# Low query parts of the prompt attention: from 64 rows in a double buffer to 128 rows, half of them zero, in a single one

## The chip, the cores and the metric

One core of one Trainium2 chip. The metric is the device time of one execution in microseconds, the median of the runs of the kernel. Each core has a matrix engine, TensorE (PE), with its own queue of weight loads (PEld), a vector engine, VectorE (DVE), a scalar engine, ScalarE (ACT), GpSimd (POOL), and SyncE (SP), which here only issues DMAs. Matrix products read SBUF (128 partitions, called rows below) and write PSUM, which this part of the kernel uses as eight banks of 128 x 512 numbers of four bytes.

## The reference, cut to what matters

One inference step of one decoder layer: a prompt of 1024 positions and 64 sample positions share the weights. A SwiGLU half step, a combined input projection, two attentions A and B over its output, their branches and an output projection, a cross attention over memory keys, a second SwiGLU half step and a final norm. The change touches the two attentions of the prompt:

```python
# A: 8 query heads over 2 key heads, keys at distances 0..128, a learned sink per head
# B: 12 query heads = 3 groups x 4 key heads; group (window, dilation) in (128,1), (512,4), (2048,16)
sc = jnp.einsum('nbqkgd,nbjkd->nbkgqj', qb, kk, preferred_element_type=jnp.float32) * ATTN_SCALE
sc = jnp.where(mask[None, :, None, None], sc, -jnp.inf)
lse = jax.nn.logsumexp(sc, axis=-1)
p = jnp.exp(sc - lse[..., None]).astype(v.dtype)
o = jnp.einsum('nbkgqj,nbjkd->nbqkgd', p, vv, preferred_element_type=jnp.float32)
```

A head has 64 features, so a score sums 64 products.

## The kernel before, in words

All matrix products run on operands split into a high and a low part of a rounded float type (F32R); a product of two numbers is the sum of high x high, high x low and low x high. `mm3` (lines 228 to 231) issues the three for the large layers. A planner (the tile framework, with a simulated time line) sets the order of the instructions on each engine: by the priority of their emission, among those that are ready in its simulation; `early(p)` emits under the earlier priority p. Engines then run their own lists in that order and wait on semaphores. Buffers of a pool with n `bufs` are reused in turn and a new use waits for the last reader of the old.

The prompt attention (lines 796 to 1034) runs over 24 units: u // 8 is the kind (0: A over its two key heads; 1 and 2: B, two key heads at a time), u % 8 the block i of 128 queries. Per unit there are two jobs, one per key head j.

- `kv_prep` (line 828) brings keys and values of 512 positions from DRAM (`zscr`), transposes the keys on PE and puts them in `KT`: 128 rows per key head, for j = 0 high parts on rows 0 to 63 and low parts on rows 64 to 127, for j = 1 the other way round.
- `q_load` (line 851) loads the raw queries of a unit by one DMA into one of four slots `qr`, which the keys and values use too.
- `q_prep` (line 860) transposes them on PE into a PSUM bank `pT` (one of three, which the jobs use for the probabilities too). For each head half e, ACT copies the high part twice (lines 873 and 874), so that a head's high part stands on rows 0 to 63 and again on rows 64 to 127; DVE subtracts it from the bank and gets the low part (lines 879 and 881), on 64 rows alone, those of the key head. All of it lies in `QT`, two buffers of 12 parts of 128 columns: 8 of high parts, 4 of low parts.
- `qk` (line 884) makes the scores of 128 queries and up to 512 keys in two products: line 890 contracts 128 rows, [high; high] with [high; low] of the keys; line 891 adds low queries x high keys over 64 rows.
- `job_a` (line 898) and `job_b` (line 941): the scores go through DVE with the mask and the maximum (`ttr`, line 463) into `Sm` (three buffers), ACT takes the exponential, in B POOL adds the groups, DVE scales, PE transposes the probabilities into `pT` (lines 930 and 982), ACT and DVE split them into `PT` (three buffers; `split2`, lines 225 and 226), and PE multiplies them with the values (`pO`).
- The unit loop (lines 1012 to 1027) emits the next unit's `q_load` and `q_prep` before the jobs of the present one, so they have priority over these.

PE's list is filled up with the gates' products (`gate`, line 801; 36 units of 24 products, tile `pf`), emitted behind all of it, some of them tied to follow a given job (`GATE_AFTER`).

Of the kernel before, what the change touches and what calls it, by code (L numbers as in the profile page):

```python
# [10 lines left out]
F32R = mybir.dt.float32r  # L11
# [23 lines left out]
G0 = 18  # L35
# Which of the attention's jobs each unit of gate work follows: their share of the units, by their length.
_SHARE = np.cumsum([1.0, 4.0] + [1.0] * 14 + ([2.0] + [1.0] * 15) * 2)
# [11 lines left out]
class Weights:  # L49
    """The stream of weight tiles in the order of their use: loads run ahead, then each is split  # L50
    exactly into a high and a low part of float32r."""

# [47 lines left out]
def trunk(ctx, tc, A, O, dbg=None):  # L100
# [8 lines left out]
    class early:  # L109
        """What is emitted inside goes before the work emitted since priority p where both are ready."""  # L110

# [9 lines left out]

    # ---------------------------------------------------------------- weights, in order of use
    entries = []
# [70 lines left out]

    # ---------------------------------------------------------------- what lives throughout
    dr = ctx.enter_context(pool(name="dr", bufs=1, space=DRAM))
# [36 lines left out]
    def finish_rstd(dst, ssum, n):  # L233
        """dst = 1/sqrt(ssum / D + eps), with a Newton step behind the square root."""
        sd = small.tile([128, 9], F32, name="sd", tag="sd")
        v = small.tile([128, 9], F32, name="vv", tag="vv")
        t = small.tile([128, 9], F32, name="tt", tag="tt")
        S.activation(sd[:, :n], ssum, AF.Sqrt, scale=1.0 / D, bias=epst)
        V.tensor_scalar(v[:, :n], ssum, 1.0 / D, EPS, op0=ALU.mult, op1=ALU.add)
        V.reciprocal(sd[:, :n], sd[:, :n])  # L240
        V.tensor_tensor(t[:, :n], sd[:, :n], sd[:, :n], op=ALU.mult)
        V.tensor_tensor(t[:, :n], t[:, :n], v[:, :n], op=ALU.mult)
        V.tensor_scalar(t[:, :n], t[:, :n], -0.5, 1.5, op0=ALU.mult, op1=ALU.add)
        V.tensor_tensor(dst, sd[:, :n], t[:, :n], op=ALU.mult)
# [33 lines left out]

    # ---------------------------------------------------------------- feed-forward
    def ffn(pre, x, psp, fp, stats, after, order=(0, 1, 2), before=lambda c: None, at=(5, 6)):  # L280
# [85 lines left out]

    # ================================================================ start, first feed-forward
    ss = const.tile([128, 1152], F32, name="ss")
# [64 lines left out]

    # ================================================================ input projection and attention
    def stop(name):
# [4 lines left out]
    with ExitStack() as ph:  # L440
# [24 lines left out]

        # ------------------------------------------------------------ projection, position-major
        m1 = ph.enter_context(ExitStack())
# [59 lines left out]

        # ------------------------------------------------------------ sample
        with early(p_m1), ExitStack() as sp_:
            # ---- scores of the widest dilation: each key serves one position  # L530
            ST = sq.tile([128, 2, 8, 2, 8], F32, name="ST")
# [17 lines left out]

            # ---- B  # L550
            with ExitStack() as sb_:
# [135 lines left out]

            # ---- A
            with pool("da") as da:
# [27 lines left out]
                for hf in range(2):  # L717
# [4 lines left out]
                    split2(KH[:, bs, 0:128], KL[:, bs, 0:128], pk[:, :].rearrange("p (b k) -> p b k", b=4))  # L722
                # per b a block of 128 query columns (b % 2, j, g, t), zero elsewhere
                QH = da.tile([128, 4, 2, 2, 2, 4, 8], F32R, name="QH")
# [70 lines left out]

        # ------------------------------------------------------------ prompt
        ap = ph.enter_context(pool("ap"))
        marks, gw = [], {}

        # ------------------------------------------------------------ gates: the work to fill in with  # L800
        def gate(u):
# [21 lines left out]
        with ExitStack() as pp:  # L823
            qe = pp.enter_context(pool("qe"))
            qp = pp.enter_context(pool("qp"))
            halves = [0]

            def kv_prep(kc, vc, hf):
                """Half of the keys of two heads, transposed: head 0 [high; low], head 1 [low; high]; values."""
                rows = slice(hf * 512, hf * 512 + 512)  # L830
# [20 lines left out]
            def q_load(i, c0, ng):  # L851
                """The queries of ng groups and two key heads, in pairs of heads."""
                qr = qe.tile([128, 4, 128], F32, name="qr", tag="qr", bufs=4)
# [6 lines left out]
            def q_prep(qr, ng):  # L860
                """Per head [high; high] over 128 rows, and per pair of heads the low parts."""
                QT = qp.tile([128, 12, 128], F32R, name="QT", tag="QT", bufs=2)
                p = bank(pst, "pT")
# [3 lines left out]
                for e in range(2):  # L867
# [7 lines left out]
                    if ng == 4:  # L875
                        for j in range(2):
                            lo = QT[j * 64:j * 64 + 64, 8:12].rearrange("p (g e) c -> p g e c", e=2)[:, :, e]
                            gs = slice(2 * j, 2 * j + 2)
                            V.tensor_tensor(lo, pv_[r, gs], _b(hi[r, gs]), op=ALU.subtract)
                    else:  # L880
                        V.tensor_tensor(QT[r, 2 * ng:3 * ng], pv_[r], _b(hi[r]), op=ALU.subtract)
                return QT

            def qk(out, QT, ng, g, j, KV, k0, n):
                r = slice(j * 64, j * 64 + 64)
                for hf in range(2):
                    a, e = max(k0, hf * 512), min(k0 + n, hf * 512 + 512)
                    if a < e:
                        o, KT, c = out[:, a - k0:e - k0], KV[hf][0], slice(a - hf * 512, e - hf * 512)
                        PE.matmul(o, QT[:, j * ng + g], KT[:, j, c], start=True, stop=False)  # L890
                        PE.matmul(o, QT[r, 2 * ng + g], KT[r, j, c], start=False, stop=True)  # L891

# [3 lines left out]

            # ---- A: sliding window with sinks
            def job_a(i, j, QT, oA, KV):
# [40 lines left out]

            # ---- B: three dilations over shared keys, two key heads at a time  # L940
            def job_b(i, j, QT, oB, KV):
# [49 lines left out]

            def qs(u):
                ph_, i = u // 8, u % 8
                if ph_ == 0:
                    return q_prep(q_load(i, 0, 4), 4)
                return q_prep(q_load(i, 640 + ph_ * 128, 3), 3)

            def kv(ph_, hf):
# [11 lines left out]
                                                ap=[[0, 128], [1, 8]]))  # L1010
            QTs = [qs(0)]
            for u in range(24):
                ph_, i = divmod(u, 8)
                if u < 23:
                    QTs.append(qs(u + 1))
                if ph_ < 2 and i == 6:
# [5 lines left out]
                for j in range(2):  # L1022
                    (job_b if ph_ else job_a)(i, j, QTs[u], ob, KVs[ph_])
                os_, t = oscr[i // 3], slice(i % 3 * 128, i % 3 * 128 + 128)
# [10 lines left out]

    # ================================================================ branches and the output projection
    xph = ctx.enter_context(ExitStack())
# [133 lines left out]

    # ================================================================ cross attention
    MS = 128.0 ** -0.5
    with ExitStack() as ph:
# [8 lines left out]
        def gbank(both):  # L1183
            """A bank for a product over all tokens; where nothing else runs, those of the scores too."""
            turn[0] = (turn[0] + 1) % 3
# [126 lines left out]
        def sample():  # L1312
            with ExitStack() as sx:
# [4 lines left out]
                with pool("dk", 2) as dk:  # L1318
# [3 lines left out]
                    for h in range(4):  # L1322
# [26 lines left out]
                        V.tensor_scalar(P[:, h], P[:, h], Z[:, h:h + 1], None, op0=ALU.mult)  # L1349
                # per b a block of 128 columns (b % 2, high or low part, h, t), zero elsewhere  # L1350
                PT = dm.tile([128, 2, 4, 2, 2, 2, 4, 8], F32R, name="PTm")
# [58 lines left out]

    # ================================================================ second feed-forward, final norm
    with ExitStack() as ph:
# [20 lines left out]
        def half(t, hf, tag):  # L1433
            """Half of the features of 128 positions, back to position-major, times the gain; their squares."""
            rows = 128 if t < 8 else 64
# [29 lines left out]
        def last(c):  # L1465
            """The second halves of the last positions and what is left of their norm, straight from PSUM."""
            ps = []
# [36 lines left out]
def constants():  # L1504
    """Tables that depend on the shapes alone."""
    f = np.float32
# [19 lines left out]
    c["c_mask"] = np.concatenate([band(2, 1, 128), band(5, 4, 512), band(8, 16, 2048)], axis=1)  # L1526
    # sample, A: rows (b % 2, j, g, t); columns: 128 cached keys, then the new keys (b, t)
    row = np.arange(128)
# [9 lines left out]
    c["c_sela"] = (cc[:, None] == np.arange(64)[None, :]).astype(f)  # L1538
    # sample, B: rows (b, h, t)
    b, t = row // 16, row % 8  # L1540
# [60 lines left out]
```

## Time and profile before

| what | us |
|---|---|
| median of 3 runs | 2725.17 (2723.47 to 2735.82) |
| profiled execution, span | 2726.0 |
| PE busy in the span | 2665.0 (98%) |
| DVE busy | 1292.6 (47%) |
| ACT busy | 835.3 (31%) |
| POOL busy | 449.1 (16%) |
| mean granted clock of PE | 0.987 of full |

The profile is of one execution. Times are microseconds from the start of the span. Busy time is the union of an engine's instructions; the ends of matrix products are modelled, so the distance between two starts tells more than a duration. "Idle before, releaser" of a group is the time in which its engine did nothing before it, and whose semaphore ended that; "issue" means that nothing was found that it waited for. The granted clock of PE has two levels, 1.00 (2.4 GHz) and 0.50 (1.2 GHz). In operand forms, 64*128 128 columns of weights on 64 rows are meant, 128*128 on 128 rows, and 128x256 is the moving operand, 128 rows by 256 columns.

The prompt attention runs from about 1150 to 1537 us.

### The profile page before, as it was taken

What the parts mean: (1) busy time and instruction counts of PE and PEld (TensorE: products, weight loads), DVE (VectorE), ACT (ScalarE), POOL (GpSimd) and SP (SyncE); (2) the same over time, 40 slices, a digit from 0 to 9 for tenths busy, and PEclk for the clock granted to TensorE, in tenths of its full rate; (3) what the DMA queues carried; (4) which work ended last, traced back from release to release, by engine and by line L of the source; (5) the groups of instructions that cost most, each with busy time, mean ns of one, the idle gap of its engine ahead of it and who ended that gap; (6) DMA issues with size and microseconds to landing.
All of it is one profiled execution on the core that took longest, in us unless ns stands there. A gap on an engine that the chain in (4) does not pass through costs nothing.

```text
span 2726.0 us, 39285 instructions
## 1 busy us (share of the span) xinstructions
PE 2665.0 (98%) x15802; PEld 2519.5 (92%) x15802; DVE 1292.6 (47%) x2694; ACT 835.3 (31%) x1585; POOL 449.1 (16%) x509
## 2 busy tenths in 40 slices
PE   8999999999999999999999899999999999999998
PEld 8999999999996688988778799898999999999998
DVE  5444444444462234467666563567444444444444
ACT  6111111111142234366545423455311111111113
POOL 1100011111126722000222142102211110000111
PEclk9999999999999999999889999999999999999999
DMA  4111111111136647422211263624511111111111
GB/s 137 39 47 47 46 41 47 47 36 43 47 104 198 228 146 219 138 77 79 64 37 48 87 182 121 197 82 131 174 40 47 47 46 41 47 47 45 41 39 66
DMA packets 239302, 231.42 MB, mean 85 GB/s; under 512 B 11688, under 2 KB 208400, under 8 KB 239120
## 3 DMA queue, kind: packets, MB, share of 16 engines
q1 hardware_dynamic: 239120, 228.91, 26.9%
q8 instruction: 124, 2.03, 0.3%
q14 instruction: 58, 0.48, 0.1%
HBM read 186.86 MB, written 42.01 MB: 84 GB/s over the span
## 4 chain that ended last, share of the span: by engine, by line
PE 89%; DVE 4%; DMA 4%; ACT 1%; issue 1%; POOL 1%; SPq 0%; DVEq 0%; POOLq 0%; ACTq 0%
PE pmm L229 19%; PE pmm L231 19%; PE pmm L230 19%; PE pS L891 2%; PE pf L229 2%; PE pf L231 2%; PE pf L230 2%; PE pb L229 2%; PE pb L230 2%; PE pb L231 2%; PE pS L890 2%; DMA qb<-zqs 1%; PE pO L230 1%; PE pO L229 1%; PE pO L231 1%; DVE xl L268 1%
## 5 line engine op out<-in xcount | busy, mean ns | idle before, releaser
L229 PE MATMUL pmm<-xh,whi 128*128 128x384 f32 (+1 forms) x2112 | 689.3, 327 | 3.2 <-DVE xo L1265 2.0
L231 PE MATMUL pmm<-xh,wlo 128*128 128x384 f32 (+1 forms) x2112 | 689.6, 327 | 0.0
L230 PE MATMUL pmm<-xl,whi 128*128 128x384 f32 (+1 forms) x2112 | 689.4, 327 | 0.0
L75 ACT ACTIVATE whi<-wraw 128x1024 fp32r<-128x1024 f32 (+2 forms) x236 | 237.9, 1021 | 741.5 <-PE pmm L230 620.3
L229 PEld LDWEIGHTS pmm<-xh,whi 128*128 128x128 f32 x2112 | 397.1, 188 | 4.1 <-ACT xh L267 4.0
L230 PEld LDWEIGHTS pmm<-xl,whi 128*128 128x128 f32 x2112 | 397.0, 188 | 0.1
L231 PEld LDWEIGHTS pmm<-xh,wlo 128*128 128x128 f32 x2112 | 397.0, 188 | 0.0
L305 POOL TENSOR_TENSOR tg<-tg,rbc 128x384 f32<-128x384 f32 x132 | 156.9, 1189 | 1367.9 <-ACT tg L304 1346.5
L327 DVE SCALAR_TENSOR_TENSOR x<-pmm,x 128x384 f32<-128x384 f32 (+1 forms) x528 | 277.9, 534 | 202.8 <-PE pmm L231 202.4
L229 PE MATMUL pmm<-hh,whi 128*128 128x384 f32 (+1 forms) x1056 | 346.4, 329 | 0.0
L231 PE MATMUL pmm<-hh,wlo 128*128 128x384 f32 (+1 forms) x1056 | 346.3, 328 | 0.0
L230 PE MATMUL pmm<-hl,whi 128*128 128x384 f32 (+1 forms) x1056 | 346.0, 328 | 0.0
L76 DVE TENSOR_TENSOR wlo<-wraw,whi 128x1024 fp32r<-128x1024 f32 (+2 forms) x236 | 279.2, 1195 | 110.4 <-ACT whi L75 109.4
L303 DVE TENSOR_TENSOR tg<-pmm,rbc 128x384 f32<-128x384 f32 x132 | 70.5, 535 | 333.9 <-PE pmm L231 333.9
L230 PEld LDWEIGHTS pmm<-hl,whi 128*128 128x128 f32 x1056 | 198.4, 188 | 0.1
L231 PEld LDWEIGHTS pmm<-hh,wlo 128*128 128x128 f32 x1056 | 198.4, 188 | 0.0
L229 PEld LDWEIGHTS pmm<-hh,whi 128*128 128x128 f32 x1056 | 198.2, 188 | 0.2
L311 DVE TENSOR_TENSOR tg<-tg,pmm 128x384 f32<-128x384 f32 x132 | 70.2, 532 | 259.0 <-PE pmm L231 254.3
L313 ACT ACTIVATE hh<-tg 128x384 fp32r<-128x384 f32 x132 | 66.2, 501 | 305.5 <-DVE tg L311 305.5
L304 ACT ACTIVATE tg<-tg 128x384 f32<-128x384 f32 x132 | 66.1, 502 | 297.3 <-DVE tg L303 297.3
L229 PE MATMUL pf<-xh,whi 128*128 128x384 f32 (+1 forms) x336 | 116.5, 347 | 2.0 <-DVE tg L814 1.9
L277 POOL TENSOR_TENSOR ss<-ss,sq 128x384 f32<-128x384 f32 (+1 forms) x63 | 71.8, 1140 | 272.4 <-ACT sq L276 265.0
(427 smaller groups left out, 4327.6 us busy)
## 6 DMA issues: line engine op xcount, KB each, us to landing
wraw<-ffn_w_gate SPq DMA_DIRECT2D x44, 512.0 KB, 3.9
wraw<-ffn_w_up SPq DMA_DIRECT2D x44, 512.0 KB, 3.9
wraw<-ffn_w_down SPq DMA_DIRECT2D x44, 512.0 KB, 4.3
wraw<-w_in SPq DMA_DIRECT2D x32, 512.0 KB, 4.3
wraw<-cache_dil_v SPq DMA_DIRECT2D x24, 512.0 KB, 4.6
k<-cache_dil_k SPq DMA_DIRECT2D x16, 512.0 KB, 5.0
zscr<-z SPq DMA_DIRECT2D x32, 256.0 KB, 4.7
qb<-zqs SPq DMA_DIRECT2D x16, 512.0 KB, 5.8
```

Of the source, the lines that this page charges most:

```text
L75: self.nc.scalar.activation(hi[:, :w], t[:, :w], AF.Copy)
L76: self.nc.vector.tensor_tensor(lo[:, :w], t[:, :w], _b(hi[:, :w]), op=ALU.subtract)
L229: PE.matmul(out, lh, rh, start=first, stop=False)
L230: PE.matmul(out, lh, rl, start=False, stop=False)
L231: return PE.matmul(out, ll, rh, start=False, stop=last)
L277: G.tensor_tensor(ss[:, d0:d0 + n], ss[:, d0:d0 + n], q[:, :n], op=ALU.add)
L303: V.tensor_tensor(t[:, :n], p[:, :n], rbc[:, c0:c0 + n], op=ALU.mult)
L304: S.activation(t[:, :n], t[:, :n], AF.Silu)
L305: G.tensor_tensor(t[:, :n], t[:, :n], rbc[:, c0:c0 + n], op=ALU.mult)
L311: V.tensor_tensor(t[:, :n], t[:, :n], p[:, :n], op=ALU.mult)
L313: S.activation(a, t[:, :n], AF.Copy)
L327: V.scalar_tensor_tensor(x[:, mo, c0:c0 + n], p[:, :n], 0.5, x[:, mo, c0:c0 + n], op0=ALU.mult, op1=ALU.add)
```

## The change

The low parts move out of `QT` (now 8 parts, two buffers still) into two tiles of their own, one per key head, `QL[0]` and `QL[1]`, each of 128 rows by four parts of 128 columns and without a second buffer. Both are filled with zeros once by POOL. `q_prep` writes the low parts on the same 64 rows as before: of key head 0 on rows 0 to 63 of `QL[0]`, of key head 1 on rows 64 to 127 of `QL[1]`; the other rows stay zero. The second product of `qk` contracts all 128 rows, low parts and zeros with the [high; low] keys.

Since the low parts have a single buffer, the unit loop prepares a unit's queries behind the jobs of the unit before, under the priority that held at the start of that unit's iteration (`early(p_u)`), and loads the raw queries one unit further ahead. The rest of the diff deletes comments.

```diff
+            QL = [qp.tile([128, 4, 128], F32R, name=f"QL{j}") for j in range(2)]
+            for t in QL:
+                G.memset(_b(t[:, :, :].rearrange("p g c -> p (g c)")), 0.0)
...
-                QT = qp.tile([128, 12, 128], F32R, name="QT", tag="QT", bufs=2)
+                QT = qp.tile([128, 8, 128], F32R, name="QT", tag="QT", bufs=2)
...
-                            lo = QT[j * 64:j * 64 + 64, 8:12].rearrange("p (g e) c -> p g e c", e=2)[:, :, e]
+                            lo = QL[j][j * 64:j * 64 + 64].rearrange("p (g e) c -> p g e c", e=2)[:, :, e]
...
-                        V.tensor_tensor(QT[r, 2 * ng:3 * ng], pv_[r], _b(hi[r]), op=ALU.subtract)
+                        V.tensor_tensor(QL[e][r, 0:ng], pv_[r], _b(hi[r]), op=ALU.subtract)
...
-                r = slice(j * 64, j * 64 + 64)
...
-                        PE.matmul(o, QT[r, 2 * ng + g], KT[r, j, c], start=False, stop=True)
+                        PE.matmul(o, QL[j][:, g], KT[:, j, c], start=False, stop=True)
...
-            def qs(u):
+            def load(u):
                 ph_, i = u // 8, u % 8
-                if ph_ == 0:
-                    return q_prep(q_load(i, 0, 4), 4)
-                return q_prep(q_load(i, 640 + ph_ * 128, 3), 3)
+                return q_load(i, 0, 4) if ph_ == 0 else q_load(i, 640 + ph_ * 128, 3)
...
-            QTs = [qs(0)]
+            QT, raw = q_prep(load(0), 4), load(1)
             for u in range(24):
                 ph_, i = divmod(u, 8)
-                if u < 23:
-                    QTs.append(qs(u + 1))
+                p_u = tc.cur_priority
...
                 for j in range(2):
-                    (job_b if ph_ else job_a)(i, j, QTs[u], ob, KVs[ph_])
+                    (job_b if ph_ else job_a)(i, j, QT, ob, KVs[ph_])
+                if u < 23:
+
+                    with early(p_u):
+                        QT = q_prep(raw, 4 if u < 7 else 3)
+                        raw = load(u + 2) if u < 22 else None
```

## Rows read from the trace of the kernel before

**Rows 1.** The page: busy us of each engine, share of the span, instructions.
```profile
PE 2665.0 (98%) x15802; PEld 2519.5 (92%) x15802; DVE 1292.6 (47%) x2694; ACT 835.3 (31%) x1585; POOL 449.1 (16%) x509
```

**Rows 2.** Busy us (instructions) by engine, three stretches of the prompt attention, clock, DMA.
```profile
1150.00:1280.00 130.00, 129.82 (x720) 109.25 (x719) 88.78 (x321) 79.85 (x211) 0.00 (x0) 1.00 0.28 85
1280.00:1410.00 130.00, 127.18 (x669) 100.27 (x667) 80.88 (x271) 68.58 (x148) 24.95 (x27) 0.88 0.19 56
1410.00:1537.00 127.00, 124.57 (x776) 99.49 (x776) 81.54 (x289) 66.32 (x132) 35.58 (x36) 0.99 0.15 46
```

**Rows 3.** Line 891: duration ns min/median/max, first and last start, forms.
```profile
L891 PE MATMUL pS<-KT,QT x228: 215/380/793, 1157.1 to 1534.9; 64*128 64x128 f32 x48, 64*128 64x256 f32 x44, 64*128 64x512 f32 x15, 64*128 64x384 f32 x7
```

**Rows 4.** Timeline, PE and its loads: start us, us, engine, line, operation.
```profile
1309.94 0.38 PE L890 MATMUL pS<-KT,QT 128*128 128x256 f32 x1
1310.25 0.18 PEld L891 LDWEIGHTS pS<-KT,QT 64*128 64x128 f32 x1
1310.25 0.38 PE L891 MATMUL pS<-KT,QT 64*128 64x256 f32 x1
1310.57 0.27 PE L229 MATMUL pO<-PT,Vh 128*64 128x128 f32 x1
```

**Rows 5.** Timeline of PE, products of 128 columns.
```profile
1362.45 0.33 PE L890 MATMUL pS<-KT,QT 128*128 128x128 f32 x1
1362.71 0.32 PE L891 MATMUL pS<-KT,QT 64*128 64x128 f32 x1
```

**Rows 6.** Timeline of PE, products that follow others of 128 rows.
```profile
1319.82 0.33 PE L231 MATMUL pf<-xh,wlo 128*128 128x384 f32 x1
1319.99 0.33 PE L229 MATMUL pf<-xh,whi 128*128 128x384 f32 x1
...
1521.06 0.98 PE L982 MATMUL pT<-ident,Sm 128*128 128x128 f32 x7
1521.80 0.31 PE L890 MATMUL pS<-KT,QT 128*128 128x128 f32 x1
```

**Rows 7.** Timeline of PE, score products grouped by kind.
```profile
1243.82 0.40 PE L890 MATMUL pS<-KT,QT 128*128 128x256 f32 x2
1244.14 0.51 PE L891 MATMUL pS<-KT,QT 64*128 64x256 f32 x3
1244.58 0.33 PE L930 MATMUL pT<-ident,Sm 128*128 128x128 f32 x1
```

**Rows 8.** The waits in the attention: us in total, times, longest.
```profile
DVE Sm L463 <- PE pS L891: 70.2, 88, 3.5
PEld pS L891 <- issue: 16.9, 74, 0.4
```

**Rows 9.** Busy us by engine and granted clock, stretches around the clock's falls.
```profile
1338.00:1344.56 6.56, 4.62 (x29) 3.68 (x28) 3.94 (x7) 6.23 (x11) 5.52 (x5) 1.00 0.02 2
1344.56:1358.22 13.66, 13.65 (x54) 10.51 (x54) 8.27 (x22) 4.91 (x11) 1.19 (x2) 0.50 0.29 84
1365.04:1382.11 17.07, 17.07 (x55) 12.32 (x55) 6.59 (x31) 4.71 (x8) 2.27 (x2) 0.50 0.03 12
```

**Rows 10.** Timeline of PE within the last of these stretches.
```profile
1366.17 0.58 PE L890 MATMUL pS<-KT,QT 128*128 128x256 f32 x1
1366.68 0.58 PE L891 MATMUL pS<-KT,QT 64*128 64x256 f32 x1
```

**Rows 11.** Timeline of all engines where one unit's queries are prepared.
```profile
1342.75 0.49 PE L865 MATMUL pT<-ident,qr 128*128 128x128 f32 x3
1344.36 0.96 PE L890 MATMUL pS<-KT,QT 128*128 128x512 f32 x3 [0.59 <-ACT QT L874]
1345.96 0.54 DVE L881 TENSOR_TENSOR QT<-pT,QT 64x384 fp32r<-64x384 f32 x1
```

**Rows 12.** Line 891 before 1340 us: first and last start are read.
```profile
L891 PE MATMUL pS<-KT,QT x98: 270/380/498, 1157.1 to 1336.4; 64*128 64x256 f32 x60, 64*128 64x128 f32 x32, 64*128 64x512 f32 x4, 64*128 64x384 f32 x2
```

**Rows 13.** Busy us by engine where DVE is densest in the first job kind.
```profile
1241.00:1293.00 52.00, 52.00 (x293) 43.56 (x292) 38.83 (x140) 36.20 (x102) 0.00 (x0) 1.00 0.28 84
```

## The prediction

> **What bounds the kernel now.** I read the page first, for the engine to follow: TensorE (PE) is marked busy for 98% of the span, the next engine, VectorE (DVE), for 47% [rows 1]. The ends of its products are modelled, though, so a busy PE can still lose time between two starts. The change touches the prompt attention only, so the second view is the busy time in the stretches in which that runs, 1150 to 1537 us: PE 381.6 of 387 us, DVE 251.2, ScalarE (ACT) 214.8 [rows 2]. No engine but PE is full there. The third view is the waits: DVE stood 70.2 us, in 88 pieces, waiting for the low score product of line 891; and the weight load of that same line stood 16.9 us in 74 pieces with nothing for it to wait for [rows 8]. So PE sets the pace of the attention, and something in line 891 holds PE.
>
> The timeline shows what. Each score is the sum of two products: line 890 contracts 128 rows, line 891 contracts 64. Of 256 columns each, they start 0.31 us apart, and what follows line 891 starts 0.32 us later [rows 4]; of 128 columns, 0.26 us apart [rows 5]. Products that follow one of the same 128 rows stand closer: 0.17 us at 384 columns, and seven of 128 columns in 0.74 us, 0.106 us each [rows 6]. By columns (0.17 x 256/384) a product of 256 should take about 0.115 us. So going from 128 rows to 64, or back, costs 0.31 - 0.115 = 0.195 us at 256 columns and 0.255 - 0.106 = 0.15 us at 128. The load of line 891 starts together with its product instead of one product ahead [rows 4], which is where the time goes: at the turn nothing overlaps. Where products of one kind stand in a group the price is lower: two of 128 rows and three of 64, all of 256 columns, take 0.76 us from 1243.82 to 1244.58 [rows 7]; five at 0.115 would be 0.575, which leaves 0.09 us for each of the two turns.
>
> Here a rule of the Trainium skill speaks against the change. "TensorE: Matmul & The Clock Gate", Part 2 (step by step), says that a weight load is pulled ahead of running products where the row groups don't conflict or it goes to the background buffer; by that the turn would cost nothing and the sum below would be zero. The row of the load at 1310.25, beside its product and not before it [rows 4], disagrees, and I go by the row.
>
> **The change, part by part.**
> *Turns taken away.* Line 891 runs 228 times [rows 3], which is also what the loops give (72 in the sliding window, 156 in the dilated attention). In the timeline 23 of them directly follow another of line 891 (one such group is in [rows 7]), so there are 205 runs of 64-row products and 410 turns. With the low parts over 128 rows, all other half zero, every turn goes; products and columns stay, and a product of 256 columns is put at 0.38 us for 64 as for 128 rows [rows 4], so the wider contraction adds nothing. The price lies between 0.09 (groups) and 0.195 us (single pairs of 256 columns). Single pairs are most of it, many of 128 columns (0.15): I take 0.16. 410 x 0.16 = 66 us; ends 410 x 0.09 = 37 and 410 x 0.195 = 80.
> *The clock.* The granted clock was 0.50 from 1344.56 to 1358.22 and from 1365.04 to 1382.11 us [rows 9]. Before the first fall PE was partly idle, 4.62 of 6.56 us busy, with waits on other engines. The second came after a run of single pairs of lines 890 and 891, with PE never idle by its records; that cause goes. At the low clock a turn at 256 columns stands 0.51 us apart [rows 10] against 0.31, so the 17.07 us would be 17.07 x 0.31 / 0.51 = 10.4 at full clock: 6.7 us back. The first fall would give 13.66 x 0.2 / 0.51 = 5.4 us, which I do not count; its wait stays. Ends: 12 us gained, or 7 us lost if new waits let the clock fall once more.
> *What becomes late next.* Without the turns the first stretch (sliding window, 72 of 228 pairs, so 66 x 72/228 = 21 us) shrinks to 109 us, in which DVE's 88.8 us are 81%; the other two shrink by 52 (the clock's 6.7 included) from 257 to 205, DVE's 162.4 us being 79% [rows 2]. Where DVE was dense and PE still never waited it was busy 38.8 of 52 us, 75%, ACT 36.2 [rows 13]. Beyond that nothing is shown. If DVE could not go above 75%, the stretches would be 118 and 217 us, and 9 + 12 = 21 us of the gain would be lost; if it can, none. I take half: 10 us.
> *Preparation of the queries moved.* The next unit's transposes, copies and subtractions are emitted behind the present unit's jobs, but with the priority of their start, so I expect them at the same place in PE's, ACT's and DVE's order. What is new is a wait: the subtractions write a single buffer per key head, and so wait for the last low product of the unit before. The trace shows room for that. In one unit the transposes start at 1342.75, the first score product follows at 1344.36 as soon as the first copies are made, and the first subtraction starts at 1345.96 [rows 11]; the last low product of the unit before had started at 1336.4 [rows 12], 9.6 us earlier. Scores run three jobs ahead of their products with the values (three buffers Sm), so the buffer is free when it is wanted. Cost: nothing. If the order slips and PE waits for one subtraction of 0.54 us [rows 11] per unit and key head, it is 46 x 0.54 = 25 us; behind the waiting subtraction on DVE stand the score maxima and the splits of the probabilities, and PE waits for these. A gain is excluded: the preparation had a second buffer before. The same wait holds one of three banks pT for longer, from the transposes to the second subtraction; it is part of that end.
> *Loads.* One DMA per unit, as before, on SP's queue, now issued one unit further ahead. The raw tiles have four slots and were issued ahead already, so nothing; the DMA share is 0.15 to 0.28 in these stretches [rows 2].
> *Memory and fills.* The double buffer shrinks by four parts of 128 columns each, the two new tiles take that much. Two fills on POOL, once, before the first subtraction; POOL is at 0.00 us in the first stretch [rows 2]. Uncovered they'd cost about two subtractions of 512 columns, by the 0.54 us for 384 some 1.4 us (estimate).
> *Products of two halves.* Products of 64 rows on different halves might run together, and that is given up. It can matter for neighbours only: 23 x 0.115 = 2.6 us at most, inside the ends. The Trainium skill, same page, Part 3, holds up just this as the way to speed up small contractions: slices on distinct row groups run at the same time, so by it 64-row products are to be kept and paired. No row of mine shows two at once, and 205 of 228 stand behind another kind, where it would give nothing.
>
> Sum: 66 + 6.7 - 10 = 63 us. The profiled execution has a span of 2726.0 us and the page gives no time around it; the median shown is 2725.17, 0.8 us lower. 2726.0 - 63 = 2663, on the scale of the median **2662 us**.
>
> **Rivals.**
> *A: the turn is not what costs.* If the 0.3 us between starts belonged to two products that accumulate on one place, or to the load, a wider contraction would change nothing: 2725 us. For it: the load of line 891 is itself as long as others. Against: the grouped products [rows 7], and the product behind line 891 is late too although it writes elsewhere [rows 4]. 6%.
> *B: DVE and ACT become the bound.* If DVE can't get above 70% over a stretch because of the chain score, maximum, exponential, scale, transpose, the first stretch needs 127 us and the others 232: gains of 3 and 25 us, 2697 us. For it: the dense stretch at 75%. Against: the 70.2 us that DVE itself spent waiting for line 891 [rows 8]. 20%.
> *C: slower.* Emitted behind the jobs, the preparation may end up behind the unit's transposes too, or hold a bank pT until they can't go on. Then at each of 23 unit changes PE has no scores ahead: from the transposes at 1342.75 to the end of the first subtraction at 1346.50 are 3.75 us [rows 11], 23 x 3.75 = 86 us, 2726 - 66 + 86 = 2746 us. It decides from 63 / 23 = 2.7 us per change on. For it: the single buffer makes the order stricter. Against: the 9.6 us of room, and the gates' products that can fill in. 7%.
> *D: all of it.* DVE follows, both falls of the clock go: 66 + 12 = 78 us, 2647 us, and with 0.195 us a turn 92 us, 2633 us. 13%.
>
> **How the numbers follow.** The forecast has the remaining 54%, with a range of its own from 2645 to 2680 us. The range for 8 in 10 leaves out C, A and the far end of D: 2634 to 2703 us. Half a per cent, 13.6 us, is about what a measurement can tell from none. Faster: the forecast, D and 18 of B's 20 parts, 0.85; within: A and 2 of B, 0.08; slower: C, 0.07.
>
> **What would show it.** Products of line 891's successor with 128 rows; pairs of 256 columns 0.11 to 0.13 us apart and loads a product ahead; no idle time put down to "issue" at these loads; the clock at 1.00 around the place of the second fall; DVE at about 80% of a shorter attention of some 325 us, and PE's waits on DVE and ACT some 10 us more. The forecast is wrong if pairs stay 0.3 us apart (A), if PE's waits in the attention grow by over 35 us (B), or if the transposes of the queries come behind those of the unit before (C).

## The result: 3.2% slower, where 2.3% faster was forecast

The changed kernel takes 2816.4 us (median of 4 runs, 2814.8 to 2819.0) against 2728.2 for the kernel before: ratio 1.0317, interval 1.0296 to 1.0339. The profiled execution's span is 2814.6 us, 88.6 more than before. This is the side of rival C. The experiments below split it in two: the wider products give some 73 us where little else changes (46 and 52 us in two other pairs of runs), and the place to which the queries' preparation moved costs 144 to 155 us.

The page of the changed kernel: PE has 12 us less of busy time than before [rows 1] in a span that is 89 us longer. In the second line, the granted clock in 40 slices, there is a hollow where the attention runs; the third is the chain that ended last, in which PE has 81% of the span.

```profile
PE 2653.3 (94%) x15802; PEld 2540.6 (90%) x15802; DVE 1307.8 (46%) x2694; ACT 840.0 (30%) x1585; POOL 448.9 (16%) x511
PEclk9999999999999999998777899999999999999999
PE 81%; DVE 5%; issue 5%; DMA 3%; ACT 3%; POOL 2%; SPq 0%; DVEq 0%; POOLq 0%; ACTq 0%
```

The window from the first score product to the last product with the values, first before, then after (length, then busy us and instructions of PE, PEld, DVE, ACT and POOL, then the granted clock):

```profile
1156.70:1551.30 394.60, 389.18 (x2258) 316.51 (x2257) 252.92 (x879) 215.07 (x490) 62.83 (x64) 0.96 0.19 58
```

```profile
1155.90:1638.40 482.50, 375.74 (x2258) 335.52 (x2258) 266.94 (x878) 222.34 (x494) 62.09 (x64) 0.84 0.16 48
```

The attention grew from 394.6 to 482.5 us, 88 us; all else kept its length. PE's time without a product rose from 5.4 to 106.8 us, and the mean clock of 0.84 means that the half level (1.2 GHz) was granted for (1 - 0.84) x 2 x 482.5 = 154 us of it, against some 32 before (the means are rounded to two places). DVE and ACT did nearly the same work as before.

What the change was to do to the products, it does. The timeline of PE after, pairs of 256 and of 128 columns:

```profile
1417.88 0.28 PE L892 MATMUL pS<-KT,QT 128*128 128x256 f32 x1
1417.88 0.19 PEld L893 LDWEIGHTS pS<-KT,QL 128*128 128x128 f32 x1
1418.00 0.28 PE L893 MATMUL pS<-KT,QL 128*128 128x256 f32 x1
...
1400.23 0.28 PE L892 MATMUL pS<-KT,QT 128*128 128x128 f32 x1
1400.35 0.27 PE L893 MATMUL pS<-KT,QL 128*128 128x128 f32 x1
1400.46 0.39 PE L229 MATMUL pf<-xh,whi 128*128 128x384 f32 x1
```

They start 0.12 and 0.11 to 0.12 us apart; in [rows 4, 5] it was 0.31 and 0.26. The weight load of the second product starts with the product before its own (1417.88). The successor of line 891 runs as often as before and contracts 128 rows:

```profile
L893 PE MATMUL pS<-KT,QL x228: 220/279/735, 1156.2 to 1623.2; 128*128 128x128 f32 x48, 128*128 128x256 f32 x45, 128*128 128x512 f32 x17, 128*128 128x384 f32 x4
```

Its weight load no longer stands without a cause: the 16.9 us of [rows 8] have no row in the waits after. In their place are these (who waited for whom, us in total, times, longest):

```profile
PE pT L984 <- DVE Sm L978: 64.6, 16, 7.5
PE pT L932 <- DVE Sm L927: 12.8, 7, 2.7
...
DVE Sm L463 <- PE pS L893: 63.7, 42, 4.9
```

PE now waits 64.6 + 12.8 us, in 23 pieces, for the scaled probabilities that it is to transpose. The timeline of one unit (block 5 of the first pair of key heads in B) shows why PE has nothing else to do meanwhile:

```profile
1402.72 0.28 PE L893 MATMUL pS<-KT,QL 128*128 128x128 f32 x1
1408.06 1.30 PE L984 MATMUL pT<-ident,Sm 128*128 128x128 f32 x5 [5.07 <-DVE Sm L978]
...
1409.99 1.07 PE L984 MATMUL pT<-ident,Sm 128*128 128x128 f32 x4
...
1412.15 0.31 PE L984 MATMUL pT<-ident,Sm 128*128 128x128 f32 x1
1412.30 0.49 PE L868 MATMUL pT<-ident,qr 128*128 128x128 f32 x3
...
1417.37 0.44 PE L892 MATMUL pS<-KT,QT 128*128 128x512 f32 x1
```

The last score of the unit starts at 1402.72. PE stands for 5.07 us until the first job's probabilities are scaled, transposes those of both jobs (line 984), and only then, at 1412.30, the next unit's queries (line 868); the next scores start at 1417.37. In [rows 11] the queries' transposes came ahead of those of the unit's own probabilities, the next scores 1.6 us behind them, and these scores filled PE while DVE, ACT and POOL worked on the probabilities. Now scores, exponentials and transposes of a unit follow one another with nothing between but what is left of the gates. The whole timeline bears this one unit out: before, the queries' transposes start ahead of all transposes of the unit before theirs at all 23 unit changes; after the change at none, at 13 they start behind all of these, at the other 10 behind all but the last one to six.

The clock around this place (length, busy us of PE, PEld, DVE, ACT, POOL, clock, DMA share):

```profile
1395.13:1405.37 10.24, 7.85 (x56) 7.08 (x54) 5.51 (x26) 3.81 (x5) 1.55 (x2) 1.00 0.07 26
1405.37:1412.20 6.83, 3.67 (x23) 3.30 (x24) 3.82 (x6) 1.69 (x5) 3.05 (x3) 0.50 0.00 0
1412.20:1429.26 17.06, 15.28 (x107) 13.74 (x106) 11.04 (x40) 8.59 (x16) 2.31 (x2) 1.00 0.17 53
```

PE was busy 7.85 of 10.24 us with a pause at the end, then came 6.83 us at 0.50, in which the transposes that everyone waits for run at the low clock. The clock fell 20 times within the attention.

### The profile page after: what moved, and what is told of

It reads as the page before. It is cut to its first block, busy times and chain, and to the rows that moved or that the text cites. A ratio compares the mean times of both kernels' runs of the same rounds, so it can differ in the third digit from the quotient of the medians.

```text
span 2814.6 us, 39297 instructions
## 1 busy us (share of the span) xinstructions
PE 2653.3 (94%) x15802; PEld 2540.6 (90%) x15802; DVE 1307.8 (46%) x2694; ACT 840.0 (30%) x1585; POOL 448.9 (16%) x511
## 4 chain that ended last, share of the span: by engine, by line
PE 81%; DVE 5%; issue 5%; DMA 3%; ACT 3%; POOL 2%; SPq 0%; DVEq 0%; POOLq 0%; ACTq 0%
PE pmm L229 18%; PE pmm L231 18%; PE pmm L230 18%; PE pb L229 2%; PE pb L230 2%; PE pb L231 2%; PE pf L229 2%; PE pf L231 2%; PE pf L230 1%; DMA qb<-zqs 1%; POOL Sm L975 1%; PE pO L229 1%; DVE xl L268 1%; PE pO L230 1%; PE pO L519 1%
## 5 line engine op out<-in xcount | busy, mean ns | idle before, releaser
L303 DVE TENSOR_TENSOR tg<-pmm,rbc 128x384 f32<-128x384 f32 x132 | 70.5, 535 | 333.8 <-PE pmm L231 333.8
L231 PE MATMUL pf<-xh,wlo 128*128 128x384 f32 (+1 forms) x336 | 117.0, 348 | 0.0
```

The costliest lines, as they stand in the source:

```text
L231: return PE.matmul(out, ll, rh, start=False, stop=last)
L303: V.tensor_tensor(t[:, :n], p[:, :n], rbc[:, c0:c0 + n], op=ALU.mult)
```

## Experiments

Theory 1: the turns cost what the prediction says, and the order of the preparation is what made the kernel slow. Rival 2: the turns cost nothing. Rival 3: the order is harmless; the wait for the single buffer of low parts costs. All ratios are to the kernel before on the same chip.

**wide_only**: wider products alone, the order left ahead of the jobs. It contracts the other key head's low parts in place of zeros.

```diff
-                        PE.matmul(o, QT[r, 2 * ng + g], KT[r, j, c], start=False, stop=True)
+                        PE.matmul(o, QT[:, 2 * ng + g], KT[:, j, c], start=False, stop=True)
```

> The kernel before with one edit: the low product contracts all 128 rows of the double buffer QT (the rows of the other key head are not zeros here, so the scores lose their meaning; the work is the same). Preparation of the queries stays ahead of the jobs. Theory 1 (turns between 64 and 128 rows cost 0.16 us each, and the order of the preparation is what made the change slow): 2728 - 63 = about 2665 us. Rival 2 (the turn is not what costs, all of the +88 us is the order): 2728 us. Rival 3 (the order is harmless, the wait for the single buffer of low parts costs): about 2665 us, as theory 1.

Measured: 2685.5 us, ratio 0.9837 (0.9817 to 0.9857), 46 us less. The window of the attention:

```profile
1155.20:1504.40 349.20, 322.79 (x2254) 297.37 (x2254) 250.21 (x877) 214.13 (x488) 63.07 (x64) 0.97 0.22 66
```

So the products gain, against rival 2, but 20 us less than theory 1 expected. PE is without a product for 26.4 of 349.2 us and the mean clock is 0.97. This kernel is not the clean test that I took it for: its low product of one key head also reads what the other half's subtraction writes, and the planner wrote another list for PE. What in that list makes PE wait was not followed up.

**order_only**: the order alone, with 64 rows and the double buffer.

```diff
...
-                if u < 23:
-                    QTs.append(qs(u + 1))
+                p_u = tc.cur_priority
...
+                if u < 23:
+                    with early(p_u):
+                        QT = q_prep(raw, 4 if u < 7 else 3)
+                        raw = load(u + 2) if u < 22 else None
```

> The kernel before with 64-row low products and the double buffer, and only the emission changed: the next unit's queries are prepared behind the jobs of the unit, under the priority of their start. Theory 1: the order costs what the change lost and what the turns gave, 88 + 63 = 151 us, so up to 2880 us; less if turns fill time in which PE would wait anyway, but not under 2816 us. Rival 2: 2816 us. Rival 3: no single buffer, no wait: 2728 us.

Measured: 2868.3 us, ratio 1.0502 (1.0483 to 1.0521), 137 us more. There is no single buffer in it to wait for, so rival 3 falls; rival 2's 2816 is missed too. The window and PE's largest wait:

```profile
1153.10:1687.40 534.30, 443.83 (x2258) 356.87 (x2257) 272.19 (x879) 222.55 (x494) 62.12 (x64) 0.80 0.14 43
```

```profile
PE pT L982 <- DVE Sm L976: 57.7, 16, 6.3
```

It is the wait seen after the change, 57.7 us in 16 pieces, here on the kernel before. From order_only to the changed kernel the attention is 52 us shorter: taking the turns away still pays, even in that pipeline.

**split**: the changed kernel, transposes and high copies emitted ahead of the jobs again, the subtractions alone (now in a function `q_low`) behind them.

```diff
...
+                if u < 23:
+                    QN, pn = q_prep(load(u + 1), 4 if u < 7 else 3)
...
                 if u < 23:
                     with early(p_u):
-                        QT = q_prep(raw, 4 if u < 7 else 3)
-                        raw = load(u + 2) if u < 22 else None
+                        q_low(QN, pn, 4 if u < 7 else 3)
+                    QT = QN
```

> The changed kernel with the preparation cut in two: transposes and high copies of the next unit emitted ahead of the jobs as in the kernel before, only the subtractions into the single buffers behind the jobs, under the priority of their start. Theory 1: scores run ahead again, 2665 us, up to 2690 us as a bank pT is held longer. Rival 2: 2728 us. Rival 3: the wait for the single buffer is still there: 2780 us or more.

Measured: 2672.3 us, ratio 0.9783 (0.9757 to 0.9809). The single buffer and its wait are in it, and it is 144 us faster than the changed kernel: theory 1. In its window PE is without a product for 14.7 us:

```profile
1153.40:1486.80 333.40, 318.72 (x2257) 292.35 (x2257) 251.31 (x880) 214.57 (x490) 62.29 (x64) 0.99 0.23 70
```

**sbank**: the changed kernel with one name replaced; the emission stays behind the jobs.

```diff
             def q_prep(qr, ng):
...
-                p = bank(pst, "pT")
+                p = bank(psS, "pS")
```

> The changed kernel with one edit: the bank of the query transposes comes from the three score banks pS and not from the three banks pT of the probabilities; the emission stays behind the jobs. Theory 1, made finer (banks pT are handed out in the order of emission, so the queries' transposes must wait for the unit's own): the queries get ahead of these, 2665 to 2710 us. If the emission behind the jobs holds them back whatever the bank: 2816 us. Rival 3: 2780 us or more.

Measured: 2660.9 us, ratio 0.9742 (0.9724 to 0.9760), 155 us faster than the changed kernel and the fastest of all, 4 us below the range of theory 1. The list around a unit change in the timeline, and the window:

```profile
1400.98 0.38 PE L984 MATMUL pT<-ident,Sm 128*128 128x128 f32 x2
1401.19 0.49 PE L868 MATMUL pS<-ident,qr 128*128 128x128 f32 x3
1401.44 0.36 PE L892 MATMUL pS<-KT,QT 128*128 128x256 f32 x1
...
1405.38 0.62 PE L892 MATMUL pS<-KT,QT 128*128 128x512 f32 x2
...
1407.13 0.49 PE L984 MATMUL pT<-ident,Sm 128*128 128x128 f32 x3
```

```profile
1157.90:1483.20 325.30, 313.24 (x2259) 288.95 (x2258) 246.44 (x879) 218.77 (x494) 62.15 (x64) 1.00 0.23 71
```

The queries' transposes (1401.19) now run before the last scores of the unit before theirs (1401.44). Their own unit's first scores start at 1405.38, and only then, from 1407.13, come the transposes of the probabilities of the unit before. The queries' transposes start ahead of all of these at 22 of the 23 unit changes, and in split at all 23. So the emission behind the jobs is not enough to hold the queries back; the bank is. One rule of the planner fits all these runs: it hands out banks of one name in the order in which the program asks for them. Asked for behind the jobs, a bank pT comes behind those of both jobs' probabilities, whatever the priority: with a priority 100000 steps earlier the planner writes the same list for PE (this was built, not run). A bank pS comes behind the unit's scores, which are done early.

**banks4**: the changed kernel with four banks pT and two pS.

> The changed kernel with four banks pT and two banks pS in place of three and three. Theory 1 (banks of one name are handed out in the order of emission): the queries' transposes still stand behind the unit's own, 2816 us or, with a score bank less, up to 2850 us. Rival 5 (three banks pT are too few, and the query bank's long hold is what costs): 2740 us or less.

```diff
-        psS = ph.enter_context(pool("psS", 3, PSUM))
-        pst = ph.enter_context(pool("pst", 3, PSUM))
+        psS = ph.enter_context(pool("psS", 2, PSUM))
+        pst = ph.enter_context(pool("pst", 4, PSUM))
```

Measured: 2813.5 us, ratio 1.0303 (1.0287 to 1.0318). The order counts, not the number: rival 5 falls. The queries' transposes start ahead of those of the unit before at none of the 23 unit changes. The window:

```profile
1163.10:1637.80 474.70, 379.15 (x2222) 330.04 (x2222) 259.92 (x879) 222.91 (x494) 61.33 (x64) 0.85 0.16 49
```

**sbank64**: sbank with 64 rows and the double buffer. PE's list holds the same products as in sbank; in the traces their order differs at 394 of 15802 places, all between 1377 and 1459 us of sbank. The edit against sbank, without the tiles' part:

```diff
-                        PE.matmul(o, QL[j][:, g], KT[:, j, c], start=False, stop=True)
+                        PE.matmul(o, QT[r, 2 * ng + g], KT[r, j, c], start=False, stop=True)
```

> As sbank (query transposes in a score bank, emission behind the jobs), but low products of 64 rows from the double buffer, as in the kernel before. Theory 1: the same pipeline with 410 turns; the difference to sbank, 2661 us, is what the turns cost: 63 us at 0.16 us each, so 2725 us (2700 to 2745 us). Rival 2: no difference, 2661 us.

Measured: 2734.1 us, ratio 1.0018 (1.0001 to 1.0035), 73 us over sbank. The traced execution took 2749.2 us, the longest of ten, so the window shows more than the median does; the load that waits for nothing stands below it:

```profile
1160.70:1566.00 405.30, 399.17 (x2258) 323.23 (x2258) 251.35 (x879) 219.81 (x494) 61.70 (x64) 0.94 0.19 57
```

```profile
PEld pS L891 <- issue: 19.8, 88, 0.4
```

In this list 430 turns at line 891 are recorded, so 73 us are 0.17 us each, what the low clock (0.94 against 1.00) adds included. Theory 1 expected 63 us in all. The turns by themselves are seen from the first score to one and the same score further on, ahead of the first fall of the clock. Up to there the two lists are equal, first sbank, then sbank64:

```profile
1157.95:1320.46 162.51, 158.88 (x1044) 146.19 (x1042) 127.99 (x470) 118.02 (x304) 10.31 (x14) 1.00 0.30 90
1160.73:1350.77 190.04, 188.01 (x1044) 153.89 (x1042) 129.84 (x470) 118.85 (x304) 10.30 (x14) 1.00 0.25 77
```

With the clock at 1.00 in both, 184 turns make 27.5 us, 0.15 us each.

**refill**: the changed kernel with more work, to see what the low clock costs. 15 of the 24 products of a gate unit run once more.

```diff
-            for k in range(KD):
+            more = 5 if u >= GF else 0
+            for s in range(more + KD):
+                k = s if s < more else s - more
...
```

> The changed kernel, and each of the 36 units of gate products that fill the attention runs 15 of its 24 products once more ahead of them, into the same bank (their sum is started anew and thrown away). That is 540 products or 36 x 2.5 = 89 us more work for PE (0.173 us at 384 columns, 0.147 at 320). Theory 1a (of the order's 149 us, 92 are PE's waits and some 57 the low clock that these waits bring): the products fall into the waits, the granted clock stays at 1.00 for most of the attention, and the kernel gets no slower or even faster: 2765 to 2820 us. Rival 4 (the low clock costs nothing, since PE waits anyway): 2816 us if the waits take all of it, up to 2905 us, whatever the clock.

Measured: 2847.5 us, ratio 1.0425 (1.0406 to 1.0444), 31 us more than the changed kernel. The window:

```profile
1157.20:1668.10 510.90, 439.99 (x2782) 403.89 (x2782) 259.76 (x877) 220.79 (x492) 61.42 (x64) 0.91 0.15 45
```

My 2765 to 2820 is missed, and the time lies within rival 4's; only a part of the added products fell into waits, of which 70.9 us remain. What rival 4 says of the clock does not follow, though: for 89 us of added products the attention grew by 28.4; the waits took 106.8 - 70.9 = 36, and the 25 left went together with the time at the low clock, which fell from 154 to 92 us. That is some 0.4 us for each us at the low clock. By that the 147 us of low clock that the changed kernel has over split would be some 59 us, and with 92 us of waits make 151 where the attention differs by 149. PE's busy time points the same way: as many products take 375.74 us after the change and 318.72 in split, 57.0 us more. The factor 0.4 is an estimate from these two runs, refill and the changed kernel, and the division that rests on it is worked out, not shown by a run.

## Why the prediction was wrong, step by step

**The step that failed** is the preparation of the queries: "so I expect them at the same place in PE's, ACT's and DVE's order", and its price, "Cost: nothing". They went behind the transposes of the unit's own probabilities, 1417.37 - 1402.72 = 14.65 us from the last score of one unit to the first of the next in the timeline above, where in [rows 11, 12] it was 1344.36 - 1336.4 = 8.0 us; PE is without a product for 5.5 us of the former and for 1.9 us of the latter. It cost 144 us (against split) to 155 us (against sbank) where nothing was put, and turned a gain into a loss. I argued from `early(p)` and from the room in [rows 11, 12] for the new wait on the low parts. That room is real: split has the wait and is fast. I did not ask which other thing the moved lines take, a bank pT, and in which order that is given out; I counted it as held for longer only.

**Rival C** named the place and, with "may end up behind the unit's transposes too", the mechanism. Its price was too small: 3.75 us per unit change were the preparation's own chain. What lies bare is the chain from the last score over maximum, exponential, sums and scale to the transposes; 144 / 23 is 6.3 us per change, with the low clock that the waits bring. And "the gates' products that can fill in" are a fixed number; they did not fill it.

**The turns** were close: 66 us, with 6.7 for the clock 72.7, against 73 measured between sbank64 and sbank, in which PE also waits some 6 us longer. The price of 0.16 us was picked from a span of 0.09 to 0.195; at full clock it measured 0.15.

**The clock**: the second fall was to go with the turns. In sbank both are gone (mean 1.00), as rival D had it for the first one, too, and so is a third, of 3.4 us from 1525.5, which the prediction passed over. In the changed kernel the waits brought 20 falls; the 7 us that I had as an end for this were far too few.

**What is late next**: the sum took off 10 us for this. In sbank DVE is busy 246.4 of 325.3 us, 76%, and PE is without a product for 12.1 us, 6.7 more than before; in split it is 9.3 more, in wide_only 21. So the term was of the right size for the change without the bank's order, and so was the whole gain: sbank is 70.5 us faster than the kernel before on its chip (2731.4), where 63 were forecast, and by the windows its attention is 69.3 us shorter. That 2660.9 stands so near the forecast 2662, and 325.3 near its "some 325 us", is in part luck: the forecast started from 2725.2 and from a stretch of 387 us, not from 2731.4 and from 394.6.

**Loads and fills**: as expected, nothing of them shows in the runs. **Rival A** fell with the spacing of 0.12 us and with sbank64. So did the reading, which the prediction set against its own, of the rule in the Trainium skill, "TensorE: Matmul & The Clock Gate", Part 2, by which the turns would have been free. The rule itself pulls a load ahead where the row groups don't conflict or it goes to the background buffer; no run shows that a turn is such a case. **Rival B** (2697 us) did not come up.

## What to carry to other kernels

Where a planner writes the order, a part that is emitted later takes its buffers later: for each moved line list the pools it draws on, PSUM banks too, and see who asked before. A priority does not help where the bank is the gate; a bank of another name, or asking earlier, does (one line: 155 us). And when a change has two halves, price and run them one by one; here the one was worth 2.6% of the time and the other cost 5%.

## What the runs showed of the hardware that was not expected

The turn between 64 and 128 rows costs 0.15 us in sbank64 at full clock, 0.17 with what the low clock adds, as read from single distances in the kernel before (0.15 to 0.195). The Trainium skill, "TensorEngine Tiling (Array Packing)", Key Properties, says that a change of the tiling mode drains TensorE; these runs agree in that every turn costs time and give the price, but that it is a drain none of them shows.

And with dense turns the clock fell: sbank64, PE without a product for 6.1 us only, has a mean clock of 0.94 in the traced execution, sbank with more idle time (12.1 us) 1.00. By the means over whole executions it is so in every run, 0.982 to 0.989 in ten of sbank64 and 0.991 to 0.994 in four of sbank. The stretch before one of the five falls in sbank64, and the stretch behind it:

```profile
1376.20:1396.20 20.00, 19.91 (x123) 15.33 (x122) 14.10 (x45) 9.56 (x19) 3.61 (x4) 1.00 0.21 64
1396.20:1399.60 3.40, 3.40 (x23) 3.40 (x23) 1.46 (x6) 1.30 (x2) 0.00 (x0) 0.50 0.09 21
```

By the records PE had a product for 19.91 of the 20 us, and the clock fell even so. A busy engine by its records was not enough here to hold the clock.
